# Memory steps ahead of the last natural block, x asked for a column group ahead, and the convolution's first stage not held

## The chip, the cores and the metric

The kernel runs on one core of a Trainium2 chip. The time is device microseconds of one launch. A core has TensorE (PE: matmuls, and PEld, the loading of their stationary operand), VectorE (DVE), ScalarE (ACT), GpSimd (POOL) and SyncE (SP). Transfers are issued by SP and by ScalarE, each in the order of its own instructions, and share 16 DMA engines. An issue that has to wait holds up what is queued behind it on its engine.

## The reference

One encoder layer for 2048 tokens of width 1024, in float32:

```python
u = _rms_norm(h, norm_mix_g[l]); proj = u @ w_in[l]          # 1024 -> 3600 columns
hy = _short_conv_centred(proj[..., :HY_COLS], hy_conv_w[l], hy_conv_b[l])
y_hy = _group_rms_norm(_hyena(hy, spec, hy_skip[l]), hy_norm_g[l], HYENA_GROUPS)
qk = jax.nn.silu(_short_conv_centred(proj[..., HY_COLS:off], ml_conv_w[l], ml_conv_b[l]))
y_ml = _group_rms_norm(_mlstm_bidirectional(qk[..., :D_MLSTM], qk[..., D_MLSTM:], ...), ml_norm_g[l], MLSTM_HEADS)
h = h + jnp.concatenate([y_hy, y_ml], axis=-1) @ w_out[l]
h = h + _cross_attention(_rms_norm(h, norm_x_g[l]), _rms_norm(mem, norm_mem_g[l]), xa_wq[l], ...)
h = h + jnp.square(jax.nn.relu(_rms_norm(h, norm_ff_g[l]) @ ff_w1[l])) @ ff_w2[l]
return _rms_norm(h, final_norm_g)
```

The Hyena part is a long convolution done twice (order 2) through a Fourier transform with filters that a small network generates; the mLSTM is a chunkwise scan in both directions; the memory has 256 tokens.

## The kernel before

All large products are split in three matmuls (`mm3`, L352 to L358): both operands are cut in a high and a low part (ScalarE casts the high part, VectorE subtracts, L365), and high × high, low × high and high × low are accumulated in one PSUM bank. PSUM banks come in two rings of four, `mm` and `hy`.

**The order.** The program is written as Python generators that yield a cost. `chain` runs one after the other, `weave(a, b, wa, wb)` advances the one that lags by yielded cost, with weights, `among(g, h, every)` puts a piece of h behind every so many pieces of g, and `take` and `beside_each` do the like. A scheduler then takes the instructions in about that order and fixes the order on each engine by its own model of the time; instructions marked with `keep_in_program_order` stay as written. What the program order says is thus a wish, and the resulting order on each engine has to be looked at.

**The stages.** Up to about 350 us the input projection of transposed column blocks (`sweep`) runs beside the filter network. From 350 to about 1165 us the Hyena convolution (`hyena`) is woven, 297 to 499, with a list `rest`: further sweeps, the blocks of columns that are projected untransposed (`natural`: for each 128 tokens 8 × 3 matmuls, then a copy to a tile `st` and a store `od<-st` or `vd<-st` from ScalarE's queue, L851, L852), the mLSTM's gates and chunk states, and then the first steps of the memory projection, with the mLSTM's first bodies beside them. From about 1240 us on attention is woven with the other mLSTM bodies, and from about 1600 us on the feed-forward network runs.

**x.** Half of the tokens (1024) lie in SBUF as `xh` and `xl`. When the last natural block of half 1 is under way, half 0 is loaded again: `prep_x(0)` sets up eight pieces of 128 × 2 × 512, four to a chunk of 512 tokens. Each is loaded by SP (L518) in one of two buffers `xn`, scaled (L507), cast and split (L365). `x_chunk` asks for one piece ahead, and only within its chunk. `natural(0, (3,))` is the first to read the new half.

**The convolution's first stage.** `spectrum(0, j2, ...)` loads two tiles (L888), transforms two groups (L177, L190), and stores two tiles `zs` of 128 × 1024 (L957, one from SP's and one from ScalarE's queue), eight times; the second stage loads them back (`a<-zs`, L905) for its matmuls L912 and L985. With `pin=2` in `beside` the group is also ordered behind the last `mm3` that was written before it (`behind`).

**The memory projection.** `memproj` has eight steps. A step projects (`project`, L674, result copied to `kt`, L676) and multiplies the step before with a second weight: four times keys (L691) and four times values (L703). Each result goes from PSUM to a tile `o` (L681, three buffers under tag `st`, which `natural` uses as well) and to DRAM by ScalarE's queue (`gd<-o`, L693; `vw<-o`, L705). The weights (`wm`, L414) come through SP's queue, up to four ahead. The scaled memory is kept in two tiles `mt` under tag `P`. `turned_in` gives back the space of x, in which the mLSTM's tiles then lie, so the mLSTM's loads (`rows<-rows`, L1210; `qn<-qt` and `kk_t<-kt`, L1215) can't start before the last matmul that reads x.

**The mLSTM.** A body computes the scores of the chunk after it (L1241), the products with the values and the states (L1279, L1281), the update of the state (L1154), the exponentials on ScalarE (L1250), and for every second body a normalisation (L1306, bank_rsqrt L217) and stores `ym<-ht`.

Of the kernel before, what the change touches and what calls it, by code (L numbers as in the profile page):

```python
# [133 lines left out]
class Prog:  # L134
# [38 lines left out]
    def beside(self, *products, pin=False):  # L173
        names = [p[0].tensor.name for p in products]
        n = min(self.banks.index(t) for t in names)
        held = self.banks[max(0, n - 4):max(0, n - 2)] if len(set(names)) > 1 else []
        b = self.nc.tensor.matmul(*products[-1], start=True, stop=True)  # L177
        if pin:
            self.tc.keep_in_program_order(b)
        if pin == 2:  # L180
            self.behind(b)
        for i in reversed(self.nc.cur_bb.bb.instructions[-4000:]):
            own = [x.bass_ap.tensor.name for x in i.ins if getattr(x, "bass_ap", None) is not None]
            for t in [t for t in held if t in own]:
                held.remove(t)
                self.tc.add_manual_dep(b.ins, i.name, mybir.DependencyInfo(
                    mybir.DependencyClass.Sync, mybir.DependencyReason.DATA), reason="beside")
        with self.tc.high_priority(2000):
            for p in reversed(products[:-1]):
                self.tc.keep_in_program_order(self.nc.tensor.matmul(*p, start=True, stop=True))  # L190
# [214 lines left out]
    def raw_stream(self, pool):  # L405
        q, items = [], list(self.mem_items)

        def load():
            w, n = items.pop(0)
            kt = w.shape[0] // 128  # L410
            t = pool.tile([128, kt, n], F32, tag=("wl", "wh")[len(items) % 2], name="wm", bufs=2)
            for k0 in range(0, kt, kt // 2):
                src = w[128 * k0:128 * k0 + 64 * kt].rearrange("(k p) c -> p k c", p=128)
                self.nc.sync.dma_start(out=t[:, k0:k0 + kt // 2], in_=src)  # L414
            q.append(t)

        load()
        load()
        yield
        while q:  # L420
            while items and len(q) < 4:
                load()
            yield q.pop(0)

    def inproj_open(self, es):
# [27 lines left out]
        items += [tr[c] for c in (4, 5, 8, 9)] + nat[:2] + tr[6:8] + nat[2:3]  # L453
        self.items, self.mem_items = items, mem

    def inv_rms(self, dst, src):
        nc, sb, n = self.nc, self.isb, dst.shape[1]
# [60 lines left out]
        self.nc.sync.dma_start(out=t, in_=src[:, 2 * j:2 * j + 2, 512 * c:512 * c + 512])  # L518
        return t

    def x_chunk(self, c):
        rb = self.spread(self.diagonal(self.rx[:, 4 * c:4 * c + 4]))
        xs = [self.x_load(c, 0)]
        for j in range(4):
            if j < 3:
                xs.append(self.x_load(c, j + 1))
            to = slice(2 * j, 2 * j + 2), slice(512 * (c % 2), 512 * (c % 2) + 512)
            self.scaled(xs.pop(0), 2 * j, self.g_mix, rb, *(t[(slice(None),) + to] for t in (self.xh, self.xl)))
            yield

    def x_first(self):
        nc, sb = self.nc, self.isb
# [91 lines left out]
    def opened(self):  # L624
        self.xes.close()
        return
        yield

    def turned_in(self):
        self.xin.close()  # L630
        return
        yield

    def prep_x(self, hf):
        self.prepq = chain(self.x_chunk(2 * hf), self.x_chunk(2 * hf + 1))

    def prep_mem(self):
        sb = self.isb
        self.memt = [sb.tile([128, 1088], F32, tag="P", name="mt", bufs=2)[:, 0:D].rearrange("p (k t) -> p k t", k=4)
                     for h in range(2)]  # L640
        self.mst = self.raw_stream(sb)
        next(self.mst)

        def load(h):
            t = sb.tile([128, D], F32, tag="xn", name="xt", bufs=2).rearrange("p (k t) -> p k t", k=4)
            self.nc.sync.dma_start(out=t, in_=self.a["mem_t"].rearrange("(k p) t -> p k t", p=128)[:, 4 * h:4 * h + 4])
            return t

        def halves():
            xs = [load(h) for h in range(2)]  # L650
            rb = self.spread(self.diagonal(self.rm))
            for h in range(2):
                for k in range(4):
                    g = self.g_mem[:, 4 * h + k:4 * h + k + 1]
                    self.nc.vector.scalar_tensor_tensor(self.memt[h][:, k], xs[h][:, k], g, rb, ALU.mult, ALU.mult)
                yield
        self.prepq = halves()

    def memproj(self):
# [8 lines left out]
        def project():  # L668
            w = next(self.mst)
            p = self.mm().rearrange("p (k t) -> p k t", k=2)  # L670
            for m in range(2):
                ms = slice(128 * m, 128 * m + 128)
                for k in range(8):
                    mul(p[:, m], w[:, k, ms], mt[k // 4][:, k % 4], start=k == 0, stop=k == 7)  # L674
            t = sb.tile([128, 4, 256], F32, tag="xn", name="kt", bufs=2)[:, 0:2]
            nc.scalar.copy(t, p)  # L676
            return t

        def staged(p):
            o = sb.tile([128, 2, 256], F32, tag="st", name="o", bufs=3)  # L680
            nc.scalar.copy(o, p)  # L681
            return o

# [142 lines left out]
    def natural(self, hf, tiles, after=None, at=4):  # L826
        nc, a, sb = self.nc, self.a, self.isb
        xh, xl = self.xh, self.xl
        win = a["w_in"][0]
        for c2 in tiles:  # L830
            n = 256 if c2 < 3 else 272
            c0 = 2560 + 256 * c2
            wh, wl = next(self.wst)
# [25 lines left out]
    def hyena(self, es):  # L859
# [89 lines left out]
        def spectrum(o, j2, z):  # L949
            st = [ta() for p in range(2)]  # L950
            for jj in range(2):
                pp = [self.hy() for b in range(2)]
                self.beside(*((pp[g], f1[own[g]], z[own[g], jj]) for g in range(2)), pin=1 if o else 2)
                for b in range(2):
                    (nc.vector.tensor_copy if b else nc.scalar.copy)(st[b][:, jj], pp[b])
            for b in range(2):
                (nc.sync if b else nc.scalar).dma_start(out=sds[o][b, :, 2 * j2:2 * j2 + 2], in_=st[b])  # L957
# [223 lines left out]
    def mlstm(self, es):  # L1181
# [824 lines left out]
def program(p):  # L2006
    with ExitStack() as ms:
        with ExitStack() as es:
# [11 lines left out]
            weave(s, f, 140, 102, True)  # L2020
            p.gates_open(es)
            n = p.memproj()
            m = p.mlstm(ms)
            with ExitStack() as hs:
                rest = chain(s, p.sweep(range(4, 10), 1, True), p.natural(1, (3, 0, 1, 2), lambda: p.prep_x(0)),
                             p.natural(0, (3,)), among(p.sweep((4, 5, 8, 9), 0, False), p.gates(), 2),
                             among(chain(p.natural(0, (0, 1)), p.sweep((6, 7), 0, False),
                                         p.natural(0, (2,), p.prep_mem, 2)), p.states(), 1),
                             p.turned_in(), take(n, 2), beside_each(n, take(m, 6)))
                weave(rest, p.hyena(hs), 499, 297, True)  # L2030
            for _ in rest:
                pass
        with ExitStack() as rs:
# [9 lines left out]
            p.ffn()  # L2043


def among(g, h, every):
    for i, v in enumerate(g):
        yield v
        if i % every == every - 1:
            next(h, None)  # L2050
    for _ in h:
        pass

# [45 lines left out]
```

## Time and profile before

| What | us |
|---|---|
| median of 3 runs | 3133.62 |
| fastest and slowest | 3127.82, 3135.12 |
| the profiled execution | 3131.11 |
| its span in the profile | 3129.0 |
| TensorE busy | 3029.1 (97%) |
| VectorE, ScalarE, GpSimd busy | 1964.8, 1489.6, 1146.9 |
| moved by DMA | 607.07 MB, 194 GB/s in the mean |

The profile lists for TensorE what ended its idle time ("waits": the waiting line, what it waited for, total, times, longest), gives the busy time of each engine in any stretch ("stretches", with the clock that TensorE was granted as a share of full speed, the busy share of the 16 DMA engines and the GB/s), follows back the chain of work that ended last, and shows each engine's rows in order of time, with the idle time before a row and what ended it in brackets. Rows of SPq and ACTq are issues of transfers, with the time that the issuing took. A row's lines are those of the kernel before.

### The profile page before, as it was taken

How to read it: one execution, taken by the hardware profiler on the slowest of the kernel's cores; microseconds unless marked ns; L12 is line 12 of the kernel's file. 1: busy time of each engine (PE TensorE's matmuls, PEld its weight loads, DVE VectorE, ACT ScalarE, POOL GpSimd, SP SyncE). 2: the span in 40 equal slices, each digit the busy share in tenths (PEclk: the TensorE clock that was granted, in tenths of full speed). 3: DMA queues.
4: the chain of work that ended last, by engine and by line, in shares of the span. 5: the costliest groups of instructions: out<-in, count | busy, mean ns of one | idle time of the engine just before them, and what ended most of it. 6: DMA issues, size and time to landing. Idle time of an engine off the chain costs nothing.

```text
span 3129.0 us, 42943 instructions
## 1 busy us (share of the span) xinstructions
PE 3029.1 (97%) x14257; PEld 2374.5 (76%) x14257; DVE 1964.8 (63%) x3448; ACT 1489.6 (48%) x2907; POOL 1146.9 (37%) x802
## 2 busy tenths in 40 slices
PE   8999999989999898999999999999999999999998
PEld 6655667766677666888887888888888878888876
DVE  7965466446646456777674656657545686555695
ACT  5443366533656225555544455556555533333335
POOL 0122012200113244324141337766456393434493
PEclk9999999999999999999999999999999999999999
DMA  6464767666878897455375657657644574434324
GB/s 212 153 210 163 235 203 220 194 215 216 241 206 249 261 316 245 145 190 186 127 268 186 217 166 243 207 178 231 205 152 153 179 234 142 152 123 152 122 91 172
DMA packets 444101, 607.07 MB, mean 194 GB/s; under 512 B 38494, under 2 KB 248542, under 8 KB 442856
## 3 DMA queue, kind: packets, MB, share of 16 engines
q1 hardware_dynamic: 405988, 546.54, 54.3%
q10 hardware_dynamic: 37892, 57.79, 5.3%
q8 instruction: 113, 1.85, 0.2%
q14 instruction: 108, 0.88, 0.1%
HBM read 401.79 MB, written 202.41 MB: 193 GB/s over the span
## 4 chain that ended last, share of the span: by engine, by line
PE 81%; DMA 7%; DVE 6%; ACT 3%; issue 2%; POOL 1%; SPq 0%; ACTq 0%; DVEq 0%; POOLq 0%
PE mm L354 17%; PE mm L358 17%; PE mm L357 17%; PE hy L358 5%; PE hy L354 5%; PE hy L357 5%; PE hy L177 3%; PE mm L912 1%; PE hy L943 1%; PE hy L985 1%; DMA xt<-in_x_t_dram 1%; DVE bl L1623 1%; PE mm L674 1%; DMA a<-hy 1%; PE mm L703 1%
## 5 line engine op out<-in xcount | busy, mean ns | idle before, releaser
L1623 DVE TENSOR_TENSOR bl<-wr,bh 128x512 fp32r<-128x512 f32 x213 | 239.8, 1132 | 132.5 <-ACT bh L1622 132.3
L1622 ACT CAST ah<-w 128x512 fp32r<-128x512 f32 x284 | 176.9, 624 | 302.5 <-PE hy L357 155.8
L365 DVE TENSOR_TENSOR wl<-wn,wh 128x512 fp32r<-128x512 f32 (+1 forms) x300 | 217.6, 772 | 102.7 <-ACT wh L365 102.4
L354 PE MATMUL mm<-xh,wh 128*128 128x512 f32 x640 | 267.7, 419 | 12.2 <-ACT wh L365 9.1
L990 POOL TENSOR_TENSOR b<-b,a 128x512 f32<-128x512 f32 x64 | 87.0, 1362 | 510.1 <-ACT b L988 320.0
L357 PE MATMUL mm<-xl,wh 128*128 128x512 f32 x640 | 255.8, 400 | 0.7 <-DVE xl L365 0.6
L1622 ACT CAST bh<-wr 128x512 fp32r<-128x512 f32 x232 | 143.8, 622 | 234.6 <-PE mm L358 176.2
L358 PE MATMUL mm<-xh,wl 128*128 128x512 f32 x640 | 255.0, 399 | 0.0
L1623 DVE TENSOR_TENSOR al<-w,ah 128x512 fp32r<-128x512 f32 x236 | 217.6, 922 | 54.9 <-ACT ah L1622 54.9
L358 PE MATMUL mm<-bh,al 128*128 128x512 f32 x576 | 224.1, 392 | 6.8 <-DVE al L1623 4.3
L354 PE MATMUL mm<-bh,ah 128*128 128x512 f32 x576 | 225.7, 392 | 0.5 <-DVE acc L1780 0.4
L357 PE MATMUL mm<-bl,ah 128*128 128x512 f32 x576 | 224.9, 390 | 0.0
L365 ACT CAST wh<-wn 128x512 fp32r<-128x512 f32 (+1 forms) x300 | 167.4, 620 | 110.4 <-PE mm L358 52.1
L357 PE MATMUL mm<-act,wh 128*128 128x512 f32 x512 | 200.5, 393 | 0.8 <-DVE act L365 0.8
L354 PE MATMUL mm<-act,wh 128*128 128x512 f32 x512 | 198.4, 393 | 1.1 <-ACT wh L365 0.9
L358 PE MATMUL mm<-act,wl 128*128 128x512 f32 x512 | 199.1, 392 | 0.3 <-DVE wl L365 0.3
L354 PE MATMUL hy<-bh,ah 128*128 128x512 f32 x448 | 175.2, 391 | 0.0
L357 PE MATMUL hy<-bl,ah 128*128 128x512 f32 x448 | 174.6, 390 | 0.0
L358 PE MATMUL hy<-bh,al 128*128 128x512 f32 x448 | 174.4, 390 | 0.0
L354 PEld LDWEIGHTS mm<-xh,wh 128*128 128x128 f32 x640 | 121.4, 190 | 67.6 <-issue 19.0
L354 PE MATMUL mm<-wh,xh 128*128 128x256 f32 (+1 forms) x512 | 155.7, 305 | 13.0 <-ACT xh L365 10.6
L336 POOL TENSOR_TENSOR b<-b 128x512 f32<-128x512 f32 x32 | 58.3, 1822 | 277.8 <-DVE b L333 137.2
(369 smaller groups left out, 8285.4 us busy)
## 6 DMA issues: line engine op xcount, KB each, us to landing
wr<-hc SPq DMA_DIRECT2D x224, 256.0 KB
w<-in_ff_w_dram SPq DMA_DIRECT2D x172, 256.0 KB
hc<-wn SPq DMA_DIRECT2D x128, 256.0 KB
wn<-in_w_in_dram SPq DMA_DIRECT2D x100, 256.0 KB
hc<-q SPq DMA_DIRECT2D x96, 256.0 KB
fs<-a SPq DMA_DIRECT2D x32, 512.0 KB
a<-fs SPq DMA_DIRECT2D x64, 256.0 KB
a<-zs SPq DMA_DIRECT2D x64, 256.0 KB
```

Of the source, the lines that this page charges most:

```text
L177: b = self.nc.tensor.matmul(*products[-1], start=True, stop=True)
L336: nc.gpsimd.tensor_tensor(e[1], f, b, ALU.subtract)
L354: first = mm(ps, lh, rh, start=start, stop=False)
L357: mm(ps, lh, rl, start=False, stop=False)
L358: self.last = mm(ps, ll, rh, start=False, stop=stop)
L365: both = (self.nc.scalar.copy(hi, src), self.nc.vector.tensor_tensor(lo, src, hi.bitcast(F32), ALU.subtract))
L674: mul(p[:, m], w[:, k, ms], mt[k // 4][:, k % 4], start=k == 0, stop=k == 7)
L703: mul(p, t[:, m, ms], o_[:, m, ds], start=m == 0, stop=m == 1)
L912: nc.tensor.matmul(pp, dm[:, m], t[:, m], start=True, stop=True)
L990: nc.gpsimd.tensor_tensor(xt, xt, hi[:, m], ALU.mult)
L1622: self.nc.scalar.copy(hi, src)
L1623: eng.tensor_tensor(lo, src, hi.bitcast(F32), ALU.subtract)
```

## The change

It has three parts; the arithmetic and the number of instructions stay, but for two activation-table loads of ScalarE that fall away.

1. The first stage's groups keep their order among the pinned instructions but are no longer held behind the `mm3` written before them, `hyena` starts with a yield of 6 in place of 24, and its weight is 279 in place of 297.
2. `x_chunks(hf)` replaces `x_chunk(c)`: eight pieces in one generator over both chunks, the first two loads issued when it is made, which is at the start of the last natural block and not in its middle, and the load of piece n + 2 asked for when piece n has been scaled.
3. `natural(0, (2,))` moves behind the first three memory steps. Its weights are loaded later (`late_w`), the memory tile is scaled in place, `kt` lies under tag `P`, `o` alternates between tags `st` (3) and `cv` (2), and the number of weights loaded ahead varies with the step. Behind it come the mLSTM's first loads, one more memory step, and the remaining steps each with a body of the mLSTM, one body fewer than before.

```diff
-        if pin == 2:
-            self.behind(b)
...
+        n = 0
         while q:
-            while items and len(q) < 4:
+            n += 1
+            if n == 4:
+                self.late_w = iter([self.weights(pool, *self.late_item, kc=2, nbufs=4)])
+            while items and n != 3 and len(q) < {2: 4, 4: 1, 5: 2}.get(n, 4):
                 load()
             yield q.pop(0)
...
-    def x_chunk(self, c):
-        rb = self.spread(self.diagonal(self.rx[:, 4 * c:4 * c + 4]))
-        xs = [self.x_load(c, 0)]
-        for j in range(4):
-            if j < 3:
-                xs.append(self.x_load(c, j + 1))
...
+    def x_chunks(self, hf):
+        parts = [(2 * hf + i, j) for i in range(2) for j in range(4)]
+        xs = [self.x_load(*p) for p in parts[:2]]
+
+        def steps():
+            rb = None
+            for n, (c, j) in enumerate(parts):
+                if j == 0:
+                    rb = self.spread(self.diagonal(self.rx[:, 4 * c:4 * c + 4]))
...
+                if n < 6:
+                    xs.append(self.x_load(*parts[n + 2]))
+                yield
+        return steps()
...
-            t = sb.tile([128, 4, 256], F32, tag="xn", name="kt", bufs=2)[:, 0:2]
+            t = sb.tile([128, 1088], F32, tag="P", name="kt", bufs=2)[:, 0:512].rearrange("p (m t) -> p m t", m=2)
...
+            turns[0] += 1
+            if turns[0] % 2:
+                o = sb.tile([128, 2, 256], F32, tag="st", name="o", bufs=3)
+            else:
+                o = sb.tile([128, 1088], F32, tag="cv", name="o", bufs=2)[:, 0:512].rearrange("p (i t) -> p i t", i=2)
...
-                if t == at and c2 == tiles[-1] and after is not None:
-                    after()
+                if c2 == tiles[-1] and after is not None:
+                    if t == 0:
+                        nxt = self.x_chunks(0)
+                    if t == at:
+                        self.prepq = nxt
...
-                self.beside(*((pp[g], f1[own[g]], z[own[g], jj]) for g in range(2)), pin=1 if o else 2)
+                self.beside(*((pp[g], f1[own[g]], z[own[g], jj]) for g in range(2)), pin=True)
...
-        yield 24
+        yield 6
...
         ld, stores = [loads(0), loads(1)], []
+        yield 1
         scores(0, ld[0])
...
-                             among(chain(p.natural(0, (0, 1)), p.sweep((6, 7), 0, False),
-                                         p.natural(0, (2,), p.prep_mem, 2)), p.states(), 1),
-                             p.turned_in(), take(n, 2), beside_each(n, take(m, 6)))
-                weave(rest, p.hyena(hs), 499, 297, True)
+                             among(chain(p.natural(0, (0, 1)), p.sweep((6, 7), 0, False, p.prep_mem), take(n, 3),
+                                         p.natural(0, (2,), wst=p.late())), st, 1),
+                             p.turned_in(), take(m, 1), take(n, 1), beside_each(n, take(m, 5)))
+                weave(rest, p.hyena(hs), 499, 279, True)
```

Lines behind the edits lie 10 to 20 higher in the changed kernel: L518 becomes L520, L693 L708, L681 L696, L691 L706, L703 L718, L1241 L1259, L1250 L1268, L1415 L1434.

On SP's queue, where the last six pieces of x for half 0 are requested (`a<-zg` and `a<-hy` are gate groups of the convolution's last stage, `wn` weights, `gt` gate columns). Before:

```order
L518 DMA xt_5637<-in_x_t_dram 128x2x512
L927 DMA a_5526<-zg0_2612 128x1024
...
L930 DMA a_5700<-hy_74 64x1024 x2
L518 DMA xt_5745<-in_x_t_dram 128x2x512
L927 DMA a_5868<-zg0_2612 128x1024
...
L930 DMA a_5872<-hy_74 64x1024 x2
...
L518 DMA xt_5747<-in_x_t_dram 128x2x512
...
L518 DMA xt_5784<-in_x_t_dram 128x2x512
L927 DMA a_6070<-zg0_2612 128x1024
...
L930 DMA a_6074<-hy_74 64x1024 x2
...
L518 DMA xt_5821<-in_x_t_dram 128x2x512
```

After:

```order
L520 DMA xt_5590<-in_x_t_dram 128x2x512
L520 DMA xt_5624<-in_x_t_dram 128x2x512
...
L945 DMA a_5899<-zg0_2612 128x1024
...
L948 DMA a_5903<-hy_74 64x1024 x2
...
L520 DMA xt_5658<-in_x_t_dram 128x2x512
L520 DMA xt_5692<-in_x_t_dram 128x2x512
...
L520 DMA xt_5784<-in_x_t_dram 128x2x512
L520 DMA xt_5821<-in_x_t_dram 128x2x512
```

The requests moved together in pairs, with one gate group between them where there were four.

On ScalarE, at the first copies and stores of the memory projection (`kt` and `o` are copies out of PSUM, `gd<-o` stores, `rw` the mLSTM's exponentials). Before:

```order
L676 COPY kt_9322<-mm_9305 128x512
L681 COPY o_9332<-mm_9327 128x512
L693 DMA gd_9234<-o_9332 128x2x256
L1250 ACT_TABLE_LOAD
L1250 ACTIVATE rw_9576<-rw_9576,cols_9543 128x128 x4
L681 COPY o_9340<-mm_9335 128x512
L1250 ACTIVATE rw_9578<-rw_9578,cols_9543 128x128 x4
L1250 ACTIVATE rw_9591<-rw_9591,cols_9543 128x128 x2
L693 DMA gd_9234<-o_9340 128x2x256
```

After, at the first keys step and then at the third:

```order
L685 COPY kt_8989<-mm_8972 128x512
L696 COPY o_8996<-mm_8991 128x512
L708 DMA gd_8839<-o_8996 128x2x256
L696 COPY o_9004<-mm_8999 128x512
L708 DMA gd_8839<-o_9004 128x2x256
...
L685 COPY kt_9617<-mm_9600 128x512
L1268 ACT_TABLE_LOAD
L1268 ACTIVATE rw_9568<-rw_9568,cols_9535 128x128 x4
L696 COPY o_9627<-mm_9622 128x512
L1166 ACTIVATE ve_9997<-va_9565,cols_9535 128x129 x4
L708 DMA gd_8839<-o_9627 128x2x256
```

The first two keys steps moved out from among the exponentials; the third now stands among them.

On TensorE, at the end of the memory projection. The first scores (L1241, L1259 after) stand in row 4100 before and 4145 after. Before, the values matmuls (L703) reach to behind the fifth scores:

```order
L1241 MATMUL hy_10168<-qn_10096,kk_t_10097 128x128 x4
...
L703 MATMUL mm_10594<-wm_10288,kt_10460 128x512 x2
L1241 MATMUL hy_10319<-qn_10249,kk_t_10250 128x128 x4
...
L703 MATMUL mm_10606<-wm_10288,kt_10460 128x512 x2
...
L1241 MATMUL hy_10490<-qn_10424,kk_t_10425 128x128 x4
...
L1415 MATMUL hy_10633<-ident_60,wn_10623 128x128 x4
```

After, they end ahead of the third:

```order
L1259 MATMUL hy_9942<-qn_9574,kk_t_9575 128x128 x4
...
L718 MATMUL mm_10374<-wm_10056,kt_10226 128x512 x2
L1259 MATMUL hy_10087<-qn_10017,kk_t_10018 128x128 x4
...
L1259 MATMUL hy_10258<-qn_10192,kk_t_10193 128x128 x4
...
L1259 MATMUL hy_10384<-qn_10339,kk_t_10340 128x128 x4
...
L1434 MATMUL hy_10529<-ident_60,wn_10519 128x128 x4
```

Two bodies more than before stand between the last values matmul and the transposes for attention (L1415, L1434 after).

More of the change, by code (lines that the diff above doesn't have):

```diff
@@ L627, in opened, with late @@
         yield
+    def late(self):
+        yield next(self.late_w)
     def turned_in(self):
@@ L649, in halves @@
         def halves():
-            xs = [load(h) for h in range(2)]
+            xs = self.memt = [load(h) for h in range(2)]
             rb = self.spread(self.diagonal(self.rm))
@@ L2043, in program, with among @@
             p.ffn()
-def among(g, h, every):
+def among(g, h, every, times=1):
     for i, v in enumerate(g):
@@ L2049, in among @@
         if i % every == every - 1:
-            next(h, None)
+            for _ in range(times):
+                next(h, None)
     for _ in h:
```

23 lines of the change are left out of this document (10 added, 13 removed).

## The prediction

> **What bounds the kernel now.** I read the busy times and the chain's shares first, then TensorE's list of waits, then the stretches where it stands idle, and last the rows of the queues at those stretches.
>
> ```profile
> span 3129.0 us, 42943 instructions
> PE 3029.1 (97%) x14257; PEld 2374.5 (76%) x14257; DVE 1964.8 (63%) x3448; ACT 1489.6 (48%) x2907; POOL 1146.9 (37%) x802
> ...
> PE mm L691 <- ACT o L681: 12.9, 2, 10.5
> PE mm L354 <- ACT xh L365: 12.2, 4, 7.5
> ...
> PE hy L1279 <- DVE bry L217: 7.5, 2, 5.8
> ...
> PE mm L674 <- ACT o L681: 2.7, 1, 2.7
> PE mm L691 <- ACT kt L676: 2.6, 1, 2.6
> ```
>
> TensorE sets the end: it is idle for 3129.0 − 3029.1 = 99.9 us in all. The change moves no work off it, so it can win only idle time and half-clock time, and lose by making more of either. The largest waits (total, times, longest) fall into three places, which these stretches show; in each row the first number behind the stretch is its length, then TensorE's busy time, and the last three are its granted clock, the DMA share and GB/s.
>
> ```profile
> 345.00:365.00 20.00, 20.00 (x91) 14.37 (x90) 8.59 (x14) 8.73 (x14) 0.00 (x0) 1.00 0.96 277
> 365.00:385.00 20.00, 20.00 (x96) 14.58 (x96) 6.67 (x11) 4.52 (x10) 0.00 (x0) 1.00 0.95 316
> 385.00:405.00 20.00, 20.00 (x85) 13.35 (x86) 11.61 (x17) 12.54 (x18) 0.00 (x0) 1.00 0.76 261
> ...
> 660.00:680.00 20.00, 11.61 (x57) 7.42 (x55) 6.97 (x12) 3.59 (x7) 0.00 (x0) 0.74 0.91 276
> 680.00:700.00 20.00, 16.71 (x102) 15.46 (x102) 8.71 (x15) 6.48 (x12) 0.00 (x0) 0.91 0.67 219
> ...
> 1030.00:1125.00 95.00, 76.19 (x352) 60.13 (x351) 33.66 (x101) 19.00 (x47) 27.38 (x24) 0.91 0.97 303
> 1204.00:1240.00 36.00, 24.15 (x143) 20.25 (x142) 20.82 (x73) 17.42 (x65) 12.49 (x10) 0.81 0.75 249
> 1085.00:1125.00 40.00, 32.25 (x132) 24.38 (x131) 16.69 (x50) 9.03 (x24) 10.51 (x8) 0.91 1.04 340
> ```
>
> The refill of x (660 to 700) idles 8.4 + 3.3 = 11.7 us. Clocks of 0.74 and 0.91 mean 10.4 + 3.6 = 14 us at half speed; what of that was not idle cost some 2 us more: about 13.5. The memory steps (1030 to 1125) idle 18.8 us, and 17 us at half clock add about 5: 24. The end of the memory projection (1204 to 1240) idles 11.9 and loses about 3 by the clock: 15. Three places hold about half of what could be won. The first convolution stage (345 to 405) has no idle time to win, at a DMA share near one.
>
> **Part 1, x a column group ahead.** The chain of waits and VectorE's last split show how the last four pieces arrive:
>
> ```profile
> 655.79 9.66 DMA xt<-in_x_t_dram
> ...
> 675.00 4.42 DMA xt<-in_x_t_dram
> ...
> 681.80 6.82 DMA xt<-in_x_t_dram
> 688.64 1.43 DVE xt L507 x2
> 690.09 1.05 ACT xh L365
> ...
> 691.17 1.23 DVE L365 TENSOR_TENSOR xl<-xt,xh 128x1024 fp32r<-128x1024 f32 x1 [1.11 <-ACT xh L365]
> ```
>
> A piece costs a load of 4.4 us on free queues or 6.8 to 9.7 beside gate loads, then 1.43 + 1.05 + 1.23 = 3.7 us of scaling and splitting. Before, pieces 4 to 7 are requested nearly one by one, with gate groups between them on SP's queue, and take 691.2 − 655.8 = 35.4 us. Changed, they stand in two adjacent pairs. I count a loaded pair (9.7), two scalings (7.4), a pair on a freer queue (4.4 to 6.8), but the second pair starts after the first scaling, so one more scaling at the end (3.7): about 26. That saves 9 of the 13.5. Bounds: 13.5 if the first request far ahead covers all, 0 if the gate group that still precedes the pairs holds them as long. I take **−9**.
>
> **Part 2, three memory steps ahead of the last natural block.** ScalarE (copies, stores) and SP (loads) explain the wait of 10.53 us:
>
> ```profile
> 1055.96 0.59 ACT L681 COPY o<-mm 128x512 f32<-128x512 f32 x1 [1.14 <-PE mm L691]
> 1077.10 0.38 ACTq L693 DMA_DIRECT2D gd<-o  x1
> 1077.51 1.28 ACT L1250 ACT_TABLE_LOAD   x1 [20.97 <-DMA qn<-qt]
> ...
> 1049.92 5.71 SPq L1210 DMA_DIRECT2D rows<-rows  x5
> ...
> 1070.51 0.66 SPq L1215 DMA_DIRECT2D qn<-qt  x1
> ...
> 1074.68 1.45 SPq L414 DMA_DIRECT2D wm<-in_xa_wk_dram  x2
> ...
> 1047.02 7.17 PE L674 MATMUL mm<-mt,wm 128*128 128x256 f32 x32
> ...
> 1080.60 5.86 PE L691 MATMUL mm<-kt,wm 128*128 128x256 f32 x16 [10.53 <-ACT o L681]
> ```
>
> The copy at 1055.96 is done in 0.59 us, but its store is issued only at 1077.10: it waits for the second qn load, which SP issues at 1070.51 behind rows and gate loads. Everything queued behind that store on ScalarE waits too, above all the copies that empty TensorE's PSUM banks. In the change the first eight copies and stores stand among natural and sweep work, with no mLSTM load to wait for, and five staging buffers replace three. But the wait isn't gone: the mLSTM loads still cannot start before the last natural matmul, and behind it the third keys step's copies now stand behind the mLSTM exponentials, and its stores behind the first qn load. Eight rows loads, two qn and kk_t pairs and the values also stand on SP ahead of the next step's weights. TensorE wants those weights after one projection and one keys step (each 32 matmul records, 7.1 us as at 1047.02: 14 us, some 17 with the state products and inverse products between). SP took 1049.92 to 1074.68, 24.8 us, from the first rows load to the next weights; without the gate groups between I count 15, and 7 for the weights to land, like qn (1070.51 to 1077.1): 22 against 17. So about 5 us stay, and 4 more for the exponentials and the clock. Of 24 go **−15**. Bounds: −22 (ScalarE never blocked) and −2 (24.8 us as before, 15 us late, plus the clock).
>
> **Part 3, what no longer stands beside the mLSTM.**
>
> ```profile
> 1204.51 1.05 PE L1241 MATMUL hy<-qn,kk_t 128*128 128x128 f32 x8
> 1205.40 0.39 PE L1279 MATMUL hy<-va,rw 128*128 128x129 f32 x2
> 1205.63 0.39 PE L1281 MATMUL hy<-cf,rw 128*128 128x129 f32 x2
> ...
> 1208.09 3.60 PE L703 MATMUL mm<-wm,kt 128*128 128x512 f32 x8
> ...
> 1214.89 1.16 PE L1241 MATMUL hy<-qn,kk_t 128*128 128x128 f32 x8 [1.42 <-DVE cf L1160]
> ...
> 1223.68 0.77 PE L1279 MATMUL hy<-va,rw 128*128 128x129 f32 x2 [5.85 <-DVE bry L217]
> ...
> 1236.33 1.16 PE L1241 MATMUL hy<-qn,kk_t 128*128 128x128 f32 x8 [0.23 <-DVE act L365]
> ```
>
> L1241 begins a body's next scores, so bodies last 10.4 and 21.4 us here; the second holds the normalisation of a pair (the 5.85 wait) and a store. A body has 24 such pairs of matmuls, 0.22 us apart, so 5.3 us. Between the first and the last scores here stand two bodies, 3.6 us of values matmuls and 16 transposes (1.8 at 0.11 each): 16.0 us, 15.8 short of the 31.8. After the change the first scores stand so late that one projection (7.2 us) and two values steps (32 records of 0.45, 14 us) are all of the memory work behind them, and three bodies then stand back to back before attention. Their matmuls, transposes included, are 17.7 us. With 10.4 + 21.4 + 10.4 = 42.2 us that leaves 24.5, so 8.7 more, and one more stretch at half clock: **+10**. Bounds: three of 10.4 us give −2, three of 21.4 give +31; DMA is freer there (0.75 and 249 GB/s), so I stay with the alternation.
>
> **Part 4, the first stage not held.**
>
> ```profile
> 353.48 0.69 PE L177 MATMUL hy<-a,f 64*128 64x512 f32 x1
> ...
> 409.54 1.98 PE L912 MATMUL mm<-a,dm 128*128 128x512 f32 x4
> ...
> 402.78 7.91 SPq L957 DMA_DIRECT2D zs<-a  x2
> ...
> 414.25 1.26 SPq L905 DMA_DIRECT2D a<-zs  x2
> ```
>
> Eight groups, each with two loads of 256 KB and two stores of 512 KB (12.6 MB together), took 353.5 to 409.5; in the new order they hold 35 us of matmuls, five of the eight nearly without other work between. The stretches 345 to 405 move 17.1 MB, so the rest needs 75 GB/s: 12.6 MB in 35 us plus 75 is 435 GB/s, against 340, the most that the rows above show. The backlog is 35 × (435 − 340)/340 = 9.8 us. The first L985, which needs all stored groups back, stands 8.4 us of matmuls behind the last group; the way from the last store to the load's issue was 3.6 us (402.78 + 7.91 to 414.25), and a load takes 4.4 or more, so 8 of the 8.4 are used without a backlog. TensorE pauses up to 10 us; groups that are ready before their stores drain cost less. I take **+4**, bounds 0 and 12.
>
> The Trainium skill (DMA: Bandwidth & Descriptors, "Where 436 GB/s comes from") gives about 358 GB/s per core as the limit for HBM transfers, beside one measured load of 16 MB at 425. By 358 the backlog would be 7.5 us, by 425 under 1, so the sum would lie 1 to 4 us lower; nothing in the rows above goes past 340.
>
> The two table loads that ScalarE saves (1.28 us each) lie beside matmuls, and the in-place scaling of the memory tile and the moved kt buffers add no instruction: 0. Without that cover the table loads would be −2.6.
>
> **Sum:** −9 − 15 + 10 + 4 = −10. Against the profiled execution's 3131.1 (span 3129.0 and 2.1 around it) that is 3121; the median of the runs, 3133.6, lies 2.5 higher, so I say **3122 us**.
>
> **Rivals.** (1) *The bodies decide, slower.* Break-even is where part 3 costs 20: three bodies of 53.5 us together, 17.8 each. For it: the 21.4 us body. Against: 10.4 beside it. At 21.4 each the sum is −9 − 15 + 31 + 4 = +11, or 3145. (2) *The memory steps stay bound by transfers.* Share 0.97 over 95 us and 340 GB/s in its second half speak for it; the idle row that names one late load speaks against. Part 2 is then 0 and the sum +5: 3136 to 3139. The Trainium skill's rule (the same page, "Issuing engines are not separate DMA queues") that all issuers share the same 16 DMA engines bears on this one: an earlier place on a queue adds no bandwidth. (3) *Both stalls vanish and nothing takes their place*: −13.5 − 22 = −35, or 3096. The DMA share of 0.75 at 1204 leaves room for it; the five groups in a row and the uncovered bodies speak against. (4) *x still arrives late*, since the pairs stand behind a gate group: part 1 is 0, −1 in all, about 3131.
>
> **How the numbers follow.** Forecast 0.36 (own range 3112 to 3131), (1) 0.21, (2) 0.18, (3) 0.15, (4) 0.10. Range 3092 to 3146: from (3) to (1). A measurement here tells 0.3%, 9.4 us, from no change: faster means under 3124.2, slower over 3143. Faster: two thirds of the forecast, (3), and a little of (4): 0.43. Slower: most of (1) and a fifth of (2), and the forecast's tail: 0.26. The rest, 0.31, is within.
>
> **What would show it.** Part 1: the xh wait of 12.2 falls to 3 to 5. Part 2: the L691 wait of 10.5 shrinks, and a wait for weights of the memory projection appears about 17 us behind the last natural matmul. Part 3: waits of the L1241, L1279 and L1154 groups grow by 9 between the last values matmul and attention. Part 4: a wait for zs or hy loads of up to 10 us near 370, where none was. I am wrong if new idle time appears elsewhere, as among the states from 740 to 1030, or if the first and third parts swap signs.

## The result

The changed kernel takes 3139.62 us (median of 14 runs, 3133.32 to 3145.19), the kernel before 3133.15 (14 runs, 3127.82 to 3137.49). The ratio is 1.0017, 95% interval 1.0010 to 1.0024; the medians differ by 6.5 us. The forecast was 3122, faster; the measured time is slower. The profiled execution took 3140.15 us. Its page begins:

```profile
span 3138.3 us, 42963 instructions
PE 3036.8 (97%) x14257; PEld 2379.9 (76%) x14257; DVE 1972.6 (63%) x3448; ACT 1483.1 (47%) x2905; POOL 1146.9 (37%) x802
```

TensorE is idle for 101.5 us where it was 99.9, and its busy time grew by 7.7 although it does the same work: more of it ran at half clock. From the list of what TensorE waited for (line, releaser, total us, times, longest) after the change, where the first row stands at the start of the kernel and was 10.0 before:

```profile
PE mm L352 <- ACT wh L363: 11.1, 3, 9.1
PE hy L1434 <- DVE act L363: 6.1, 3, 4.9
PE mm L930 <- DMA a<-fs: 5.5, 1, 5.5
PE hy L1298 <- DVE bry L215: 4.9, 1, 4.9
...
PE hy L177 <- DVE cb L1178: 4.1, 1, 4.1
PE hy L1172 <- ACT ht L1312: 3.9, 3, 3.2
PE hy L1003 <- DMA a<-zs: 3.7, 3, 3.1
...
PE mm L352 <- ACT xh L363: 3.2, 2, 1.8
...
PE mm L683 <- DMA wm<-in_xa_wv_dram: 1.4, 2, 1.0
```

The waits of 10.5 for `o` and 7.5 for `xh` are gone, and several of 3 to 6 us stand in their place. The stretches that the prediction used, in the changed kernel (length, busy time of PE, PEld, DVE, ACT and POOL, then clock, DMA share, GB/s):

```profile
365.00:385.00 20.00, 20.00 (x88) 11.57 (x87) 9.44 (x16) 8.08 (x14) 0.00 (x0) 1.00 1.03 363
385.00:405.00 20.00, 14.48 (x48) 6.81 (x49) 5.41 (x9) 4.08 (x8) 0.00 (x0) 0.83 0.77 268
660.00:680.00 20.00, 20.00 (x136) 15.89 (x136) 11.82 (x19) 6.87 (x12) 0.00 (x0) 1.00 0.85 275
680.00:700.00 20.00, 14.90 (x77) 11.39 (x72) 12.61 (x20) 6.59 (x10) 0.00 (x0) 0.83 0.76 258
1030.00:1125.00 95.00, 89.04 (x486) 72.03 (x485) 37.71 (x112) 29.21 (x66) 29.06 (x25) 0.98 0.84 269
1204.00:1240.00 36.00, 25.68 (x143) 23.07 (x143) 27.56 (x90) 18.87 (x68) 14.94 (x12) 0.74 0.68 222
```

At 1030 to 1125 TensorE gained 12.9 us of busy time. Where it went shows only when the whole span is laid out. Two stretches that the prediction left out, before the change:

```profile
750.00:900.00 150.00, 146.71 (x722) 102.65 (x722) 100.14 (x235) 85.14 (x144) 22.63 (x17) 1.00 0.72 220
1300.00:1600.00 300.00, 298.58 (x1587) 253.43 (x1586) 213.88 (x551) 166.33 (x466) 81.32 (x60) 1.00 0.54 179
```

and after it:

```profile
750.00:900.00 150.00, 142.64 (x668) 100.64 (x667) 101.29 (x237) 83.56 (x142) 23.44 (x17) 0.99 0.68 203
1300.00:1600.00 300.00, 294.46 (x1580) 249.83 (x1579) 210.62 (x534) 165.75 (x472) 82.18 (x62) 0.99 0.53 174
```

Each lost some 4 us of busy time, and some clock. To compare kernels I use one number for each stretch, **lost time**: TensorE's idle time, and half of the time that it worked at half clock, summed over pieces of 4 us. With a granted clock of c, 2 × (1 − c) of a piece counts as half clock, and half of what of that exceeds the piece's idle time is added. The span less the lost time is 3008.6 to 3015.2 us in all fourteen kernels, so the measure accounts for nearly all by which their profiled spans differ. Where a stretch's work is the same in two kernels, the difference is what the edit costs there. All kernels of this study, in us (columns: b before, a changed; the others are the experiments below):

```
              b      a    p1_stage p1_free p1_rate p1_weight p1_yield   p2_x  p3_mem p3_six p13_nox p23_held phase_mid phase_ahead
   0- 200   24.5   27.7     23.1    24.0    23.9     23.7     24.8      28.2    22.9   24.1    23.7    26.8     23.5      23.6
 340- 450    0.0    7.8      7.6     0.0     7.7      0.0     11.5       0.0     0.0    0.0     6.8     0.0      0.0       0.0
 600- 750   15.9    7.8      7.9    15.9     5.1     12.3      7.3      15.0    16.4   16.7     4.0    17.7      2.5       5.4
 750- 900    3.3    8.9      9.3     4.1     8.1      7.3     12.9       3.0     4.0    4.1    10.2     3.8     13.4      15.4
1000-1150   25.5    8.2     21.7    25.1    21.7     14.4     12.4      25.6    12.8   14.0     4.7    14.7     23.0      13.3
1150-1300   17.2   23.8     20.2    17.5    18.3     52.0     19.5      19.1    24.1   31.9    24.5    24.1     17.3      19.4
1300-1600    1.4    6.7      1.6     1.2     1.6      1.5      1.3       1.7     6.9    1.4     8.1     6.8      1.6       1.8
whole span 118.1  126.6    122.0   119.3   118.0    141.9    122.0     124.7   118.7  126.2   118.8   127.1    115.8     111.9
```

Two kernels with the same work in a stretch agree there to about 1 us (b and p1_free, for example). Each column is one profiled execution. In the kernels that move no body beside attention nothing behind 1600 is edited, and yet the sums there lie between 26.6 and 30.8, so a difference of the last row below 5 us says little, and the timed runs decide.

### The profile page after: what moved, and what is told of

The parts are those of the page before. It is cut to its first block, busy times and chain, and to the rows that moved or that the text cites. A ratio compares the mean times of both kernels' runs of the same rounds, so it can differ in the third digit from the quotient of the medians.

```text
span 3138.3 us, 42963 instructions
## 1 busy us (share of the span) xinstructions
PE 3036.8 (97%) x14257; PEld 2379.9 (76%) x14257; DVE 1972.6 (63%) x3448; ACT 1483.1 (47%) x2905; POOL 1146.9 (37%) x802
## 4 chain that ended last, share of the span: by engine, by line
PE 82%; DMA 7%; DVE 6%; ACT 2%; issue 2%; POOL 1%; SPq 0%; ACTq 0%; DVEq 0%; POOLq 0%
PE mm L356 17%; PE mm L352 17%; PE mm L355 17%; PE hy L352 6%; PE hy L356 6%; PE hy L355 6%; PE hy L177 3%; PE mm L930 2%; PE hy L961 2%; PE hy L1003 1%; DMA xt<-in_x_t_dram 1%; PE mm L683 1%; DMA gd<-o 1%; PE hy L1172 1%; PE mm L718 1%
## 5 line engine op out<-in xcount | busy, mean ns | idle before, releaser
L355 PEld LDWEIGHTS mm<-xl,wh 128*128 128x128 f32 x640 | 122.0, 191 | 52.3 <-issue 25.0
```

What stands on the lines that cost most here:

```text
L355: mm(ps, lh, rl, start=False, stop=False)
```

## The experiments

**p1_stage, the first part alone.**

```diff
-        if pin == 2:
-            self.behind(b)
...
-                self.beside(..., pin=1 if o else 2)
+                self.beside(..., pin=True)
...
-        yield 24
+        yield 6
...
-                weave(rest, p.hyena(hs), 499, 297, True)
+                weave(rest, p.hyena(hs), 499, 279, True)
```

> The kernel before with the first part alone: the first stage's groups not held, the first yield 6, the weight 279; x and the memory steps as before. Theory A (each part loses or wins at its own place only): TensorE waits some 6 us for a<-fs or a<-zs near 395, and the time is 7 to 9 us longer, about 3141. Theory B (an earlier convolution also meets the chunk states worse): the stretch 750 to 1000 loses 5 to 6 us more as well, 12 to 15 us in all, about 3147. If the wait near 395 needs the other parts, the time stays within 3 us of before.

Measured: 3132.98 us, ratio 0.9996 (0.9988 to 1.0005). The 7.6 at 340 to 450 and 6.0 more at 750 to 900 came, as theory B has it, but so did the gain at the refill of x, 15.9 to 7.9, and 3.8 at 1000 to 1150, less 3.0 at 1150 to 1300. By the timed runs the part gives and takes the same amount; both theories had it slower.

**p2_x, the second part alone.**

```diff
-    def x_chunk(self, c):
+    def x_chunks(self, hf):
...
-                rest = chain(s, p.sweep(range(4, 10), 1, True), p.natural(1, (3, 0, 1, 2), lambda: p.prep_x(0)),
+                rest = chain(s, p.sweep(range(4, 10), 1, True), p.natural(1, (3, 0, 1, 2), True),
```

> The kernel before with the x pieces alone (one generator of eight pieces, two ahead). Theory A: the stretch 600 to 750 loses 7 to 9 us less, 0 to 200 loses 2 to 4 more (pieces of half 1), in all 4 to 6 us shorter, about 3128. Theory B (the shorter wait came from the earlier convolution, whose gate groups stand elsewhere on SP's queue): the wait of L354 for xh stays above 9 us and the time within 3 us of before.

Measured: 3136.75 us, ratio 1.0010 (1.0001 to 1.0018). Theory B at the refill, which still loses 15.0, with a wait for `xh` of 10.4 in two pieces; 3.7 more are lost ahead of 200, and the time is 3.8 longer, a little more than it allowed. Asking for the pieces in pairs is not what the changed kernel gains at the refill. SP's issues there (start, time of the issue), first of this kernel, then of p1_stage, where x is asked for with the old code:

```profile
646.96 1.58 SPq L518 DMA_DIRECT2D xt<-in_x_t_dram  x2
652.10 2.79 SPq L938 DMA_DIRECT2D a<-zg  x2
654.94 1.12 SPq L941 DMA_DIRECT2D a<-hy  x2
...
656.78 0.51 SPq L518 DMA_DIRECT2D xt<-in_x_t_dram  x1
...
668.58 0.37 SPq L518 DMA_DIRECT2D xt<-in_x_t_dram  x1
...
675.95 0.37 SPq L518 DMA_DIRECT2D xt<-in_x_t_dram  x1
...
682.52 1.00 SPq L518 DMA_DIRECT2D xt<-in_x_t_dram  x1
```

```profile
631.63 1.40 SPq L925 DMA_DIRECT2D a<-zg  x2
...
634.30 1.21 SPq L925 DMA_DIRECT2D a<-zg  x2
...
655.99 2.27 SPq L516 DMA_DIRECT2D xt<-in_x_t_dram  x2
...
663.51 0.89 SPq L925 DMA_DIRECT2D a<-zg  x2
...
668.17 2.10 SPq L516 DMA_DIRECT2D xt<-in_x_t_dram  x2
...
681.65 1.58 SPq L516 DMA_DIRECT2D xt<-in_x_t_dram  x2
```

With the second part alone the last four requests are still single, with gate groups (`a<-zg`, `a<-hy`) from 652 on in between. With the first part alone they stand in pairs, and two gate groups have gone ahead of them, from 631 on.

**p3_mem, the third part alone,** with its buffers and the late weights.

```diff
-                             among(chain(..., p.sweep((6, 7), 0, False),
-                                         p.natural(0, (2,), p.prep_mem, 2)), p.states(), 1),
-                             p.turned_in(), take(n, 2), beside_each(n, take(m, 6)))
+                             among(chain(..., p.sweep((6, 7), 0, False, p.prep_mem), take(n, 3),
+                                         p.natural(0, (2,), wst=p.late())), st, 1),
+                             p.turned_in(), take(m, 1), take(n, 1), beside_each(n, take(m, 5)))
```

> The kernel before with the memory steps alone (steps ahead of the last natural block, buffers, one mLSTM body fewer before attention). Theory A: the stretch 1000 to 1150 loses 15 to 19 us less, 1150 to 1300 loses 5 to 8 more, and 1300 to 2200 some 7 more, since one more body runs beside attention: 2 to 5 us shorter, about 3130. Theory B (what was lost behind 1300 is chance or comes from the other parts): 8 to 12 us shorter, about 3123.

Measured: 3134.72 us, ratio 1.0000 (0.9992 to 1.0009). The memory steps lose 12.7 us less, 1150 to 1300 loses 6.9 more and 1300 to 1600 5.5 more: 12.7 − 12.4, nothing. Theory A in where the losses stand, with a smaller gain than it had, and the part's whole gain is given back within 500 us.

**p23_held, the changed kernel with the first part undone.**

```diff
+        if pin == 2:
+            self.behind(b)
...
-                self.beside(..., pin=True)
+                self.beside(..., pin=1 if o else 2)
...
-        yield 6
+        yield 24
...
-                weave(rest, p.hyena(hs), 499, 279, True)
+                weave(rest, p.hyena(hs), 499, 297, True)
```

> The changed kernel with the first stage held as before (x pieces and memory steps changed, first part undone). Theory A: it lacks the 8 us lost at 350 to 450 and is 6 to 10 us faster than the kernel before, about 3125. Theory B (the 6 us lost between 750 and 1000 come from the memory steps): 0 to 4 us faster, about 3131.

Measured: 3138.74 us, ratio 1.0010 (1.0001 to 1.0019). Both theories were too fast: without the first part the refill loses 17.7 again. The 5 to 6 us at 750 to 900 are gone with it (3.8), so they don't come from the memory steps.

**p1_free, only the hold removed.**

```diff
-        if pin == 2:
-            self.behind(b)
...
-                self.beside(..., pin=1 if o else 2)
+                self.beside(..., pin=True)
```

> The kernel before with the hold of the first stage's groups removed and nothing else: the first yield stays 24 and the weight 297. Theory A (taking the hold away bunches the groups; the wait at 340 to 450 is the price of the bunching): 5 to 8 us are lost at 340 to 450, and the refill of x still loses 14 to 17 us between 600 and 750, since the later convolution keeps its place; 6 us slower, about 3139. Theory B (the earlier convolution, not the bunching, makes the wait): nothing lost at 340 to 450, and the time as before.

Measured: 3135.80 us, ratio 1.0005 (0.9995 to 1.0015). Theory B: no stretch up to 1600 changes by more than 1 us. The hold does nothing here.

**p1_rate, only the first yield 6 and the weight 279, the hold kept.**

```diff
-        yield 24
+        yield 6
...
-                weave(rest, p.hyena(hs), 499, 297, True)
+                weave(rest, p.hyena(hs), 499, 279, True)
```

> The kernel before with the first yield 6 and the weight 279, the hold kept. Theory A (the refill of x is freed by the convolution's other phase, its gate groups standing elsewhere on SP's queue): 600 to 750 loses 7 to 9 us as in the first part alone, 340 to 450 nothing, 750 to 900 some 9: about 2 us faster than before, 3131. Theory B (the hold decides the phase as well): 600 to 750 loses 14 to 17 us as before.

Measured: 3133.75 us, ratio 0.9995 (0.9986 to 1.0005). Loss and gain of the first part are all here, at 340 to 450 too, where I had expected nothing. The chain of waits of this kernel (start, time, what), its SP issues, a stretch, the first matmul of the first stage's last group, and a row each of the waits of TensorE and of SP from 340 to 420 show the loss:

```profile
384.13 6.68 DMA a<-fs
390.94 3.75 PE mm L912 x4
```

```profile
383.44 1.29 SPq L897 DMA_DIRECT2D a<-fs  x2
...
388.46 12.46 SPq L957 DMA_DIRECT2D zs<-a  x2
```

```profile
370.00:390.00 20.00, 15.56 (x66) 7.80 (x65) 7.17 (x12) 6.21 (x11) 0.00 (x0) 0.96 1.00 358
```

```profile
397.86 0.69 PE L177 MATMUL hy<-a,f 64*128 64x512 f32 x1
```

```profile
PE mm L912 <- DMA a<-fs: 5.4, 1, 5.4
...
SPq L957 <- DVE a L955: 15.6, 5, 10.4
```

TensorE has seven of the first stage's eight groups done by 385.6, where before the seventh was done at 402.0 and the eighth at 409.6. The queues are full (share 1.00, 358 GB/s), and the filter that L912 needs, asked for from 383.4 on, lands at 390.8; TensorE waits 5.4 us for it. The eighth group stands behind that wait, at 397.9. SP's row of 12.46 us holds two stores: the first takes 1.67 us, the second is issued at 400.6, once VectorE has copied the eighth group, and SP waits 10.4 us for that copy in between.

**p1_weight and p1_yield, the second of these two edits alone and the first alone.**

> The kernel before with the weight 279 alone; hold and first yield 24 stay. Theory A (the earlier start by the first yield packs the first stage; the weight moves the later stages): nothing lost at 340 to 450, and 600 to 750 loses 5 to 9 us in place of 16: 5 to 8 us faster than before. Theory B (the first yield alone sets the phase everywhere): as before in all stretches, within 2 us.

> The kernel before with the first yield 6 alone; hold and weight 297 stay. Theory A: 6 to 9 us lost at 340 to 450 for a<-fs, and 600 to 750 loses 10 to 17 us: 4 to 8 us slower than before. Theory B: the table of the first part, that is 7 to 8 lost at 340 to 450 and 5 to 8 at 600 to 750, the time as before.

Measured: the weight alone 3156.72 us (4 runs), ratio 1.0077 (1.0047 to 1.0106); the yield alone 3138.73 us, 1.0013 (1.0002 to 1.0025). Neither theory held for the weight. It lets the convolution lag: its first gate group at the refill comes at 670 us in place of 649, its last store at 1234 in place of 1174, beside the mLSTM, and 1150 to 1300 loses 52.0 in place of 17.2. The yield alone brings the loss at 340 to 450 (11.5) and the gain at 600 to 750 (7.3 left), so theory B in kind, but with a larger loss and a longer time. The convolution is then still ahead at the memory steps (the last stage's gate groups of the second order begin at 1023, where it was 1034), and these lose 12.4 in place of 25.5 with the third part undone.

**p3_six, p3_mem with one more piece of the mLSTM ahead of attention.**

```diff
-                             p.turned_in(), take(m, 1), take(n, 1), beside_each(n, take(m, 5)))
+                             p.turned_in(), take(m, 1), take(n, 1), beside_each(n, take(m, 6)))
```

> The memory steps alone, with the sixth body of the mLSTM kept ahead of attention. Theory A (the 5 us lost at 1300 to 1600 are the price of the body that moved beside attention): 1300 to 1600 loses 1 to 2 us as before, while 1150 to 1300 loses another 6 to 16 us, since a fourth body is uncovered: the same to 8 us slower than the memory steps alone, 3132 to 3141. Theory B (the loss at 1300 to 1600 has another cause): 1300 to 1600 still loses 6 to 7.

Measured: 3134.97 us, ratio 0.9998 (0.9988 to 1.0007). Theory A: 1300 to 1600 is back at 1.4, and 1150 to 1300 pays 7.8 more. The body costs 5 to 8 us on either side.

**p13_nox, the changed kernel with x asked for as before.**

```diff
-    def x_chunks(self, hf):
+    def x_chunk(self, c):
...
-                rest = chain(s, p.sweep(range(4, 10), 1, True), p.natural(1, (3, 0, 1, 2), True),
+                rest = chain(s, p.sweep(range(4, 10), 1, True), p.natural(1, (3, 0, 1, 2), lambda: p.prep_x(0)),
```

> The changed kernel with x asked for as before (first and third part only). Theory A (the x pieces bring nothing at the refill, which the first part frees, and cost 3 to 4 us at 0 to 200): 600 to 750 loses 7 to 9 us, 0 to 200 some 23, and the time is 3 to 5 us shorter than the changed kernel's 3139.6, about 3135. Theory B (the pieces are needed together with the first part): 600 to 750 loses 12 or more and the time is as changed or longer.

Measured: 3137.24 us, ratio 1.0002 (0.9993 to 1.0012), against 1.0017 (1.0010 to 1.0024) with the second part; the intervals overlap a little. Theory A: 600 to 750 loses only 4.0, 0 to 200 is back at 23.7. Added up, the three parts alone make −0.0004 + 0.0010 + 0.0000 = +0.0006. The 0.0011 that the changed kernel has beyond that, 3.4 us, is within what the four intervals leave open, so it is not shown that the parts work on each other.

**phase_mid and phase_ahead, only the pace of the convolution changed,** built on the kernel before to see whether the phase alone (how far the convolution is ahead of the work woven with it) explains the refill, and whether its gain can be had without its price.

```diff
-                yield 4.6
+                yield 5.7 if o else 3.5
```

That is phase_mid; phase_ahead has `yield 4.6 if o else 3.5` there.

> The kernel before (all three parts undone) with only the convolution's pace changed: the yields of its second stage are 3.5 in place of 4.6 in the first order and 5.7 in the second, so that the first stage keeps its place, the gate groups come some 18 us earlier at the refill of x, and the rest is back in its old phase. Theory A (the refill's wait depends on the phase of the gate groups alone): 340 to 450 loses nothing, 600 to 750 loses 5 to 9 us in place of 16, 750 to 900 some 3 to 6: 6 to 9 us faster than before. Theory B (the wait depends on more than the phase): 600 to 750 loses 13 to 17, the time as before.

> As the run with the changed pace, but the second order keeps 4.6, so that the convolution stays ahead to its end. Theory A: 600 to 750 loses 5 to 9 us, 750 to 900 some 9 to 13 as with the first yield 6, 1000 to 1150 some 12 to 15 in place of 25.5, since fewer gate groups meet the memory steps: 8 to 14 us faster than before. Theory B: what is won at 600 to 750 and 1000 to 1150 is lost again at 750 to 900 and 1150 to 1300, the time within 3 us of before.

Measured: phase_mid 3135.01 us, ratio 0.9997 (0.9989 to 1.0006); phase_ahead 3132.95 us, 0.9990 (0.9981 to 0.9999). The refill loses 2.5 and 5.4 in place of 15.9, and the first stage nothing: the phase it is, as theory A of both has it. But the time is theory B's, since 750 to 900 now loses 13.4 and 15.4 in place of 3.3, where the second order's first stages meet the sweeps of half 0, with waits like these of phase_ahead (line, releaser, total, times, longest):

```profile
PE hy L943 <- DVE b L991: 3.6, 3, 2.3
PE mm L791 <- DVE a L916: 3.3, 1, 3.3
PE mm L912 <- DMA a<-fs: 2.0, 1, 2.0
```

phase_ahead, with the gain of 12 us at the memory steps, is the one kernel here that is faster than the kernel before, by 0.1%, an amount at the edge of its interval.

## Why the prediction was wrong

**Part 1 (x, −9): the size was right, the cause wrong.** The refill lost 8.1 us less in the changed kernel (of 15.9 before, where I had counted 13.5). But I took the pairs on SP's queue, which I read from the order of the whole changed kernel, for the work of `x_chunks`. p2_x has no gain, p13_nox has all of it without `x_chunks`, and phase_mid has 13.4 with the pace alone. What freed the refill is the phase; the queue's rows show it as gate groups of the convolution that go ahead of the requests.

**Part 2 (memory steps, −15): right.** 25.5 fell to 8.2, so 17.3; 12.7 belong to the third part alone. The rest is mostly the pace (3.8 in p1_stage). The earlier place of the steps is not the only way to this gain: with the steps where they were, the pace alone brings 13.1 in p1_yield and 12.2 in phase_ahead. The term that I kept was too large: from the first rows load to the next weights I counted 15 us, and a wait of 5.

```profile
1093.38 6.80 SPq L1228 DMA_DIRECT2D rows<-rows  x8
1100.22 0.45 SPq L1233 DMA_DIRECT2D qn<-qt  x1
...
1105.17 1.69 SPq L412 DMA_DIRECT2D wm<-in_xa_wv_dram  x2
```

```profile
1110.82 1.97 PE L683 MATMUL mm<-xt,wm 128*128 128x256 f32 x8 [0.99 <-DMA wm<-in_xa_wv_dram]
```

It took 11.8 (1093.38 to 1105.17). The wait for weights stands where it was forecast, some 18 us behind the last natural matmul (1092.5), but is 1.4 us in two pieces. The exponentials did stand in front of the third keys step's copies, as predicted, without TensorE noticing.

**Part 3 (bodies, +10): the sum near, 6.6 measured, the wait another.** TensorE's rows of the changed kernel, where L1259 begins a body's next scores:

```profile
1188.52 1.05 PE L1259 MATMUL hy<-qn,kk_t 128*128 128x128 f32 x8
...
1195.44 1.16 PE L1259 MATMUL hy<-qn,kk_t 128*128 128x128 f32 x8 [0.70 <-DVE cf L1178]
...
1203.33 0.77 PE L1298 MATMUL hy<-va,rw 128*128 128x129 f32 x2 [4.89 <-DVE bry L215]
...
1213.34 1.91 PE L1259 MATMUL hy<-qn,kk_t 128*128 128x128 f32 x8
...
1228.51 1.12 PE L1434 MATMUL hy<-ident,wn 128*128 128x128 f32 x4 [4.91 <-DVE act L363]
1229.41 1.91 PE L1259 MATMUL hy<-qn,kk_t 128*128 128x128 f32 x8
```

The three bodies last 6.9, 17.9 and 16.1 us, 40.9 together where I had 42.2: one body alternates with the next, and the normalisation's wait (4.89) stands in the second. Less the 17.7 of matmuls that leaves 23.2, 7.4 more than the 15.8 before, where I had 8.7. But the waits that should have grown did not: those of the L1241, L1279 and L1154 groups add up to 11.7 us from 1150 to 1300 before, and to 12.0 after. What grew is the wait of the transposes for attention, which before was

```profile
PE hy L1415 <- DVE act L365: 1.3, 1, 1.3
```

and after it the 4.91 in the rows above; with their smaller waits the transposes waited 1.9 us and then 5.9. The half clock cost 3.5 and then 5.8. That the sum came out near is in part luck.

**Part 4 (first stage, +4): mis-sized, 7.8 measured, with the wrong edit and the wrong load.** The backlog was there, but TensorE did not wait near 370 for `zs` or `hy`. It waited 5.5 us near 390 for `a<-fs`, the second stage's first filter, which my account of the stage leaves out, and then worked at half clock: the four matmuls that waited took 3.75 us, where they took 1.98 before. SP asks for that filter at 387.2, behind the groups' loads, and it is under way for 7.46 us. In the 4.4 of a load on free queues it would have landed some 3 us earlier (an estimate), so the full queues make about half of the wait, and the late request the rest. The hold that I blamed does nothing (p1_free); the first yield makes the packing (p1_yield, p1_rate). The changed kernel moved 363 GB/s from 365 to 385, more than the 340 that I took as the most, and p1_yield moved 395 from 1100 to 1120. With 363 the working gives a backlog of 6.9 us in place of 9.8 (an estimate), so the backlog's size is not why the loss was larger. The Trainium skill (DMA: Bandwidth & Descriptors, "Where 436 GB/s comes from") gives about 358 as the limit per core for HBM transfers. The traces don't agree with it as a limit: 395 over 20 us goes past it.

**The sum: here the prediction failed.** The four terms came to −10 and measured −8.1 − 17.3 + 6.6 + 7.8 = −11.0. That these agree is luck in part, by what was said of parts 1, 3 and 4. What I put at nothing without saying so is the rest of the span: +5.6 at 750 to 900, which the pace brings (p1_stage, p1_rate and p1_yield have it, p2_x and p3_mem don't); +5.3 at 1300 to 1600, the body that moved beside attention (p3_six takes it away); +3.2 ahead of 200, the pieces of half 1 (p2_x has 3.7); and +5.4 behind 1600 in this one execution. Of these last, 1.9 lie at 1600 to 2000, where the kernels with the moved body lose 2.9 to 4.6 and all others 1.3 to 2.4; no experiment assigns the rest. That is 19.5, and the stretches that the table leaves out give −0.2: −11.0 + 19.3 = +8.3, the 8.5 of the last row. The two profiled spans differ by 9.3, the medians of all runs by 6.5. The prediction named 740 to 1030 as a place where new idle time would prove it wrong, and gave it no price. The account of the change says "one body fewer than before", and the prediction did not ask what that body would meet beside attention.

**Rivals.** The first, bodies that decide, was not it: they cost less than forecast. The second, memory steps bound by transfers, fell with the 17.3; that its time, 3136 to 3139, is the nearest to the measured one is chance. The third, that both stalls vanish and nothing takes their place, was half right: the refill's loss halved and that of the memory steps fell by two thirds, but new losses elsewhere took their place. The fourth holds for the edit in `x_chunks` by itself (p2_x), not for the kernel.

**Open.** Why the pieces of half 1 cost 3 to 4 us ahead of 200, with VectorE busy for 160 of the 200 us there, wasn't tried; nor what makes the losses at 750 to 900. TensorE's longest wait there is for a load in the changed kernel (`a<-zs`, 3.1 us) and for VectorE in phase_ahead. What the changed kernel loses behind 2000 is open too.

## What to carry to other kernels

A gain seen in a combined change's order belongs to no single edit until each has run alone: here the pairs on the queue came from a pacing constant, not from the code written for them. Where one engine is busy 97% of the time, moving work out of a stall puts it beside other work with limits of its own, so price the place that it moves to, over the whole span, and not just the place that it leaves. A part can be worth nothing with 13 us won in one stretch: lay out lost time by stretch, as above, and the two halves show.

## What the runs showed of the hardware

A long row of a queue need not be a slow issue. SP's two stores in p1_rate stand in one row of 12.46 us, but the first took 1.67 us and the second waited for its data. While SP waited, the DMA share (the last number but one) fell to nothing:

```profile
388.00:392.00 4.00, 1.06 (x2) 0.57 (x3) 0.00 (x0) 0.00 (x0) 0.00 (x0) 0.53 1.04 415
392.00:396.00 4.00, 4.00 (x10) 2.18 (x9) 0.00 (x0) 0.00 (x0) 0.00 (x0) 0.61 0.49 198
396.00:400.00 4.00, 4.00 (x18) 2.16 (x17) 0.81 (x2) 0.67 (x2) 0.00 (x0) 1.00 0.00 0
```

The same rows show what a pause costs TensorE beyond its length. After the wait of 5.4 us, which ended at 390.9, the granted clock was 0.53 and 0.61 in the pieces up to 396 and 1.00 in the next; 340 to 450 lost 2.0 us by the clock beside 5.7 idle.
